# Attention by pairs of heads, masks merged into other operations, the normalisation on ScalarE and all convolution taps on VectorE

## The chip, the cores and the metric

The kernel runs on one core of one Trainium2 chip. The metric is the device time of one execution in microseconds (us). Before the change three runs took 2025.07, 2022.62 and 2021.49 us, a median of 2022.62. Engines are called as in the profile: PE is TensorE's matmuls and PEld its weight loads, DVE is VectorE, ACT is ScalarE, POOL is GpSimd, SP is SyncE.

## The reference

Two layers of a transformer block over 256 tokens `x` and 256 context tokens, width 1024, all in float32. What it computes, without the helpers:

```python
for l in range(DEPTH):
    last = l == DEPTH - 1
    mx, mc = ...                  # nine modulation vectors for x and for the context
    x = x + 0.5 * mx[2] * swiglu(modulate(rms_norm(x, norm_g[l, 0]), mx[0], mx[1]), w_ffn1_gu[l], w_ffn1_down[l])
    ...                           # the same for the context
    zx = modulate(rms_norm(x, norm_g[l, 1]), mx[3], mx[4]) @ w_in[l]
    zc = modulate(rms_norm(h_ctx, norm_g[l, 1]), mc[3], mc[4]) @ w_in[l]
    qa, ka, va, qb, kb, vb, ux, gx = split_combined(zx)
    qa_c, ka_c, va_c, qb_c, kb_c, vb_c, uc, gc = split_combined(zc)
    qb, kb = apply_axial_rope(qb, cos, sin), apply_axial_rope(kb, cos, sin)
    ya = neighborhood_attention(qa, ka, va, ka_c, va_c, na_rpb[l], rows)
    yb = window_attention(qb, kb, vb, kb_c, vb_c, sw_sink[l])
    yc = conformer_conv(ux, conv_dw_w[l], conv_dw_b[l], conv_ln_g[l], conv_ln_b[l])
    x = x + mx[5] * merge_branches(ya, yb, yc, gx, b_gate[l], w_out_a[l], w_out_b[l], w_out_c[l], w_out[l])
    if not last:
        ...                       # context_attention, the same convolution and merge for the context
    x = x + 0.5 * mx[8] * swiglu(modulate(rms_norm(x, norm_g[l, 2]), mx[6], mx[7]), w_ffn2_gu[l], w_ffn2_down[l])
return rms_norm(x, final_g)
```

The change lies in the middle, between `zx` and `merge_branches`. The neighborhood attention has six heads of 64 features; a query sees a window of 8 by 16 places with a bias `na_rpb` and all context keys. The window attention has six query heads on two key heads, sees keys at most 128 tokens away and the context, and has one more logit, `sw_sink`, in the softmax. The convolution is depthwise over 256 channels with 31 taps, then a layer norm over the channels and silu. Each branch goes through its own projection and a sigmoid gate before the common `w_out`.

## The kernel before

Features lie on the 128 partitions and tokens along the columns: 256 of x, then 256 of the context (in the last layer the queries, gates and the convolution are needed for x alone, 256 columns). Every float32 product is made of three matmuls of rounded parts, `hi*hi`, `hi*lo` and `lo*hi` (`mm3`, L317 to L321). The weights come in one stream from DRAM in the order of use; a block of 512 columns, four weight tiles, is split into `wh` by ACT (L125) and `wl` by DVE (L126) shortly before PE needs it.

`middle(l, norm, nxt)` is the middle branch of one layer. Its work on PE, in the order of the program:

- the first blocks: the keys `ka` of the neighborhood heads and the two halves of the convolution's input, which are put into a padded tile (`hp`);
- the values: eight k of twelve products of 512 columns (`v`), each k followed by `CV_PACE[l]` steps of the convolution;
- two queries (`query`), then the loop over units. A unit is a head and `u`: the first or the second 128 queries of x, or, in layer 0, the 256 queries of the context (`u == 2`). For each unit come the scores (`qk`), the softmax (`soft`), later the transposes of the weights (`turn`, 4 products into the bank `pt`) and, after a head's last unit, the products with the values (`pv`). Between them `step(n)` takes n steps from `fill`, a chain of the other blocks of the middle: the third query, the keys and queries of the window heads with their rotation, a few gates, and `merge(b, f)`, which projects branch b (2 is the convolution, 0 the neighborhood heads, 1 the window heads) and multiplies it by its gate. A step is three matmuls. The turn of a unit comes `LOOKAHEAD` units after its scores.

The scores of a head are one product on all 128 rows, which stacks two parts of the key or of the query, and one on 64 rows for the third part (L1024). The softmax takes a maximum on DVE (L1036, L1037 with the mask or bias), the exponential with its sum on ACT (L1057), the reciprocal on DVE (L1066) and the scaling of the weights on POOL (L1068). Biases `tb` come by DMA for each head, and POOL adds the window's mask (L1004).

`conv()` has 62 taps of 31 per half of the channels. 44 are done on DVE (L802, L805), the last 18 of one half on ACT (a product, L811) and POOL (a sum, L815, with a last sum on L817). Then comes its layer norm: the mean (`cmean`, L827), sums of squares (`sums`), the inverse root spread over all rows (`rstd`), scaling, tanh and the split parts `ych` and `ycl`. Work of the norm that waits for other engines is put off by `after(n, fn)` until n further ticks, and `flush()` runs what is left when `fill` needs the result.

A scheduler places the instructions on each engine in an order of its own guess, within what the data allow; the tiles come from rings and pools of fixed size.

Of the kernel before, what the change touches and what calls it, by code (L numbers as in the profile page):

```python
# [39 lines left out]
# columns of the packed vectors  # L40
# [31 lines left out]
LOOKAHEAD = 2  # L72
N_TAP = 6
# [5 lines left out]
N_ROT = 4  # L79
# [3 lines left out]
N_CPOOL = 18  # L83
CV_PACE = (3, 2)
EARLY = (2, 8)
# [4 lines left out]
def dit_block_kernel(ctx, tc, xT, vec, ident_d, const, crow, gfin, rpb, ws, ada0, adaT, out):  # L90
    """Builds the program; returns the 128x128 weight tiles (input, layer, first row, first column)
    in the order in which ws has to hold them."""
# [78 lines left out]
    def mod_chunk(l, ch, ks=slice(0, KD)):  # L171
        """What the chunk of eight feature tiles is for, from the modulation itself."""
# [22 lines left out]
    def ada_first(ch, raws):  # L195
        """A chunk of layer 0's first two, on TensorE, in two halves."""
# [25 lines left out]
    class Ada:  # L222
        """The modulation's other feature tiles, one after the other on VectorE."""
# [41 lines left out]
    class Stream:  # L265
# [14 lines left out]
        def make(self):  # L280
            """Loads and splits the next tiles."""
# [66 lines left out]
    def inv_rms(groups, nq, unit, out, new=S):  # L348
        """inv_root along the columns, on all partitions. In two steps, for TensorE to work in between."""
# [14 lines left out]
    class Norm:  # L364
        """rms_norm(R) * g * (1 + scale) + shift. Its first products are taken of R * g * (1 + scale)
        with the shift as one more column, and scaled by 1/rms afterwards."""
# [76 lines left out]
        def parts(self, p):  # L443
            """(product without its shift, columns, shift) for each set."""
# [53 lines left out]
    class FirstNorm(Norm):  # L498
        """The program's first norm, made while the modulation comes in: its first products are taken
        of all but the shift and 1/rms, and the shift's own product is added afterwards."""  # L500
# [19 lines left out]
        def blocks(self, fns):  # L520
# [54 lines left out]
            # the shift's product: its two parts are the columns of the stationary operand, and a last  # L575
            # product turns the rows into columns and adds the parts
# [36 lines left out]
    def project(l, br, name, xs, sets, nxt, bg=lambda f: 0):  # L613
        """R += gate * (xs @ w), and what the next norm needs of R."""
        for f in range(KD):
# [4 lines left out]
            if f == KD - 2:  # L620
                # the function's table is there before the norm needs it
# [3 lines left out]
    def ffn(l, br, norm, nxt, ada_end=None):  # L625
        """ada_end: how many of the modulation's tiles there have to be at the end."""
# [11 lines left out]
        def bg(i):  # L638
            """The tiles to do now, of 20 pairs of blocks and the first 6 tiles of the projection."""
# [40 lines left out]
    def middle(l, norm, nxt):  # L680
# [7 lines left out]
        def pair(name):  # L688
            """A split tile of the width of qs."""
# [9 lines left out]
        mna = ph[:, C_MNA:C_MNA + GRID_W]  # L699
        msw = ph[:, C_MSW:C_MSW + 2 * NX].rearrange("p (u k) -> p u k", u=2)  # L700
# [6 lines left out]
        # on the first blocks: the keys of the neighborhood heads and one half of the convolution's input  # L707
# [4 lines left out]
        for parts in fb[:3]:  # L712
            # a tile for each head: the one part where its rows are, the rest in the other half
            kt = [S(F32R, "ka") for _ in range(2)]
            for t, sl, b in parts:
                for s, r in enumerate(rows):
                    o = rows[1 - s]
                    nc.scalar.activation(out=kt[s][r, sl], in_=t[r], func=AF.Identity, bias=b[r])
                    nc.vector.scalar_tensor_tensor(
                        out=kt[s][o, sl], in0=t[r], scalar=b[r], in1=f32(kt[s][r, sl]),  # L720
                        op0=ALU.add, op1=ALU.subtract)
            ka.append(kt)
# [26 lines left out]
        # the other half of the convolution's input  # L749
# [587 lines left out]
```

## Time and profile before

| | |
|---|---|
| three runs, median | 2022.62 us (2021.49 to 2025.07) |
| profiled execution, span from the first to the last instruction | 2022.2 us |
| granted TensorE clock over the span, mean | 0.993 |
| middle branch of layer 0 up to its `w_out` | about 441 to 788 us |
| middle branch of layer 1 up to its `w_out` | about 1598 to 1800 us |

No time other than its span is given for the profiled execution. The profile names a group by line, engine, operation and tiles (out<-in), with the count, the busy time and the mean of one. A timeline row is start, length, engine, line, operation, tiles, count and in brackets the idle time before it with what ended it. A matmul's length includes the pipeline's depth, so a series is timed from start to start. The granted clock is the share of full speed that PE had in a stretch.

### The profile page before, as it was taken

What the parts mean: (1) busy time and instruction counts of PE and PEld (TensorE: products, weight loads), DVE (VectorE), ACT (ScalarE), POOL (GpSimd) and SP (SyncE); (2) the same over time, 40 slices, a digit from 0 to 9 for tenths busy, and PEclk for the clock granted to TensorE, in tenths of its full rate; (3) what the DMA queues carried; (4) which work ended last, traced back from release to release, by engine and by line L of the source; (5) the groups of instructions that cost most, each with busy time, mean ns of one, the idle gap of its engine ahead of it and who ended that gap; (6) DMA issues with size and microseconds to landing.
All of it is one profiled execution on the core that took longest, in us unless ns stands there. A gap on an engine that the chain in (4) does not pass through costs nothing.

```text
span 2022.2 us, 29714 instructions
## 1 busy us (share of the span) xinstructions
PE 1973.9 (98%) x10650; PEld 1658.4 (82%) x10650; DVE 1466.8 (73%) x3330; ACT 921.4 (46%) x1828; POOL 222.5 (11%) x220
## 2 busy tenths in 40 slices
PE   7999999997999999999999999999999989999998
PEld 3788888895777788988888888888888978999998
DVE  5887777579976655887667659766774899978654
ACT  4533323355655544543333335333333757767553
POOL 0000000107322200100000010000001233200001
PEclk9999999998999999999999999999999989999999
DMA  7455555421221222254544524544453243355553
GB/s 286 166 191 178 174 178 176 137 83 54 71 98 63 76 92 94 94 188 152 171 156 156 176 96 165 162 157 163 156 166 119 70 130 104 135 180 186 188 184 109
DMA packets 82516, 287.22 MB, mean 142 GB/s; under 512 B 9152, under 2 KB 10944, under 8 KB 81984
## 3 DMA queue, kind: packets, MB, share of 16 engines
q1 hardware_dynamic: 79488, 277.91, 41.5%
q0 software_dynamic: 864, 4.78, 0.6%
q10 hardware_dynamic: 2016, 2.64, 0.5%
q8 instruction: 83, 1.36, 0.3%
q14 instruction: 65, 0.53, 0.1%
HBM read 284.24 MB, written 1.05 MB: 141 GB/s over the span
## 4 chain that ended last, share of the span: by engine, by line
PE 89%; DVE 8%; ACT 1%; issue 1%; POOL 0%; DMA 0%; ACTq 0%; DVEq 0%; POOLq 0%
PE g L320 13%; PE g L319 13%; PE g L321 13%; PE pr L319 8%; PE pr L321 8%; PE pr L320 8%; PE b L321 3%; PE b L319 3%; PE b L320 3%; DVE cacc L805 2%; PE f L319 2%; PE sc L1024 2%; PE f L320 2%; PE f L321 2%; PE pt L1078 1%; DVE wl L126 1%
## 5 line engine op out<-in xcount | busy, mean ns | idle before, releaser
L125 ACT ACTIVATE wh<-raw 128x512 fp32r<-128x512 f32 x760 | 472.8, 629 | 712.1 <-PE g L320 261.7
L126 DVE TENSOR_TENSOR wl<-raw,wh 128x512 fp32r<-128x512 f32 x760 | 533.2, 706 | 166.5 <-PE pr L321 89.5
L246 DVE CUSTOM_DVE_ANT_0 junk<-araw,phase 128x512 f32<-128x512 f32 x512 | 356.1, 696 | 144.8 <-DMA araw<-in_adaT_dram 135.2
L320 PE MATMUL g<-Hl,wh 128*128 128x512 f32 (+1 forms) x1248 | 457.8, 367 | 1.7 <-DVE Hl L480 1.7
L321 PE MATMUL g<-Hh,wl 128*128 128x512 f32 (+1 forms) x1248 | 457.6, 367 | 0.0
L319 PE MATMUL g<-Hh,wh 128*128 128x512 f32 (+1 forms) x1248 | 457.4, 367 | 0.0
L320 PEld LDWEIGHTS g<-Hl,wh 128*128 128x128 f32 x1248 | 234.8, 188 | 43.3 <-DVE Hl L480 2.2
L321 PEld LDWEIGHTS g<-Hh,wl 128*128 128x128 f32 x1248 | 234.5, 188 | 42.0
L319 PEld LDWEIGHTS g<-Hh,wh 128*128 128x128 f32 x1248 | 234.6, 188 | 41.5
L319 PE MATMUL pr<-gh,wh 128*128 128x512 f32 (+1 forms) x704 | 258.5, 367 | 0.0
L321 PE MATMUL pr<-gh,wl 128*128 128x512 f32 (+1 forms) x704 | 257.6, 366 | 0.0
L320 PE MATMUL pr<-gl,wh 128*128 128x512 f32 (+1 forms) x704 | 257.4, 366 | 0.0
L387 POOL TENSOR_TENSOR sq<-sq,sq 128x512 f32<-128x512 f32 (+1 forms) x36 | 44.0, 1222 | 1277.9 <-ACT sq L380 1275.8
L321 PE MATMUL b<-Hh,wl 128*128 128x512 f32 (+1 forms) x480 | 167.7, 349 | 10.6 <-DVE wl L126 10.5
L319 PE MATMUL b<-Hh,wh 128*128 128x512 f32 (+1 forms) x480 | 171.0, 356 | 0.0
L320 PE MATMUL b<-Hl,wh 128*128 128x512 f32 (+1 forms) x480 | 166.4, 347 | 0.0
L321 PEld LDWEIGHTS pr<-gh,wl 128*128 128x128 f32 x704 | 132.4, 188 | 23.5
L320 PEld LDWEIGHTS pr<-gl,wh 128*128 128x128 f32 x704 | 132.4, 188 | 23.2
L319 PEld LDWEIGHTS pr<-gh,wh 128*128 128x128 f32 x704 | 132.4, 188 | 23.0
L319 PE MATMUL f<-qh,wh 128*128 128x258 f32 (+1 forms) x400 | 121.1, 303 | 0.1
L320 PE MATMUL f<-ql,wh 128*128 128x258 f32 (+1 forms) x400 | 116.6, 292 | 0.0
L321 PE MATMUL f<-qh,wl 128*128 128x258 f32 (+1 forms) x400 | 116.5, 291 | 0.0
(234 smaller groups left out, 2819.3 us busy)
## 6 DMA issues: line engine op xcount, KB each, us to landing
raw<-in_ws_dram SPq DMA_DIRECT2D x380, 512.0 KB, 3.4
araw<-in_adaT_dram SPq DMA_DIRECT2D x128, 512.0 KB, 3.9
araw<-in_ada_dram SPq DMA_DIRECT2D x32, 256.0 KB, 5.9
phase<-in_crow_dram POOLq DMA_DIRECT2D x3, 1024.0 KB, 6.0
tb<-in_rpb_dram ACTq DMA_DIRECT2D x12, 192.0 KB, 2.4
R<-in_xT_dram SPq DMA_DIRECT2D x8, 256.0 KB, 5.3
phase<-in_const_dram POOLq DMA_DIRECT2D x2, 544.0 KB, 5.8
out_dram<-fin SPq DMA_DIRECT2D x4, 256.0 KB, 2.5
```

Of the source, the lines that this page charges most:

```text
L125: nc.scalar.activation(out=hi, in_=src, func=AF.Copy)
L126: nc.vector.tensor_tensor(out=lo, in0=src, in1=f32(hi), op=ALU.subtract)
L246: nc.vector.tensor_tensor_reduce(out=junk, in0=raw[:, c], in1=self.rows[:, s, c], scale=1.0, scalar=0.0, op0=ALU.mult, op1=ALU.add, accum_ ...
L319: nc.tensor.matmul(ps, wh, xh, start=start, stop=False)
L320: nc.tensor.matmul(ps, wh, xl, start=False, stop=False)
L321: nc.tensor.matmul(ps, wl, xh, start=False, stop=stop)
L387: eng.tensor_tensor(out=a[:, full], in0=a[:, full], in1=sq[:, full], op=ALU.add)
L805: nc.vector.scalar_tensor_tensor(out=wide(acc), in0=x, scalar=w, in1=wide(acc), op0=ALU.mult, op1=ALU.add)
L1024: nc.tensor.matmul(o, a[:, c], b[:, k], start=i == 0, stop=i == 1)
L1078: nc.tensor.transpose(pt[:, i * P:(i + 1) * P], pf[:, i * P:(i + 1) * P], ident)
```

## The change

The heads are handled in pairs. The query and key of two heads are one split pair of tiles, one head on rows 0 to 63 and one on rows 64 to 127; the scores are three products on 64 rows for each head, with the two heads taking turns into two PSUM banks. There are 216 such products rather than 72 on 128 rows and 72 on 64; the other counts of matmuls stay. Queries are scaled by the negative factor, so a minimum takes the place of the maximum, and the exponential has the scale -1. The neighborhood mask is put into the bias table on the host, and ACT negates the table after its load (L972). For the window heads the mask has zeros for the context, so one operation covers all 512 columns (L1009). The normalisation goes from POOL to ACT (L1032). A pair's transposes come at `u == 1` (16 in a row) and `u == 2` (8), each bank split in one operation of 512 columns; the values' products come for both heads, and the output is split once a pair.

All 62 taps are done on DVE (L788, L791), one step a k beside the values (`CV_V`) and one every second step of `fill` after that (`CV_PACE`). Several gates are made ahead, before the keys and queries of the window heads (`EARLY`: 7 in layer 0, 16 in layer 1), in layer 1 two to a tile. `LOOKAHEAD` goes from 2 to 1. Comments are dropped, which shifts the line numbers.

```diff
-C_MNA = C_SIN + NX
-C_MSW = C_MNA + GRID_W
-C_N = C_MSW + 2 * NX
+C_MSW = C_SIN + NX
+C_N = C_MSW + 3 * NX
...
-LOOKAHEAD = 2
-N_TAP = 6
+LOOKAHEAD = 1
+N_TAP = 3
...
-N_ROT = 4
+N_ROT = 2
...
-N_CPOOL = 18
-CV_PACE = (3, 2)
-EARLY = (2, 8)
+CV_V = (1, 1)
+CV_PACE = (2, 2)
+EARLY = (7, 16)
...
-                if m % 2 and m // 2 < N_CPOOL:
-                    # the last taps of one half, on ScalarE and GpSimd
-                    x, w = tap(1, nv + m // 2)
-                    t = S(name="cside") if side is None else next(taps)
-                    nc.scalar.activation(out=wide(t), in_=x, func=AF.Copy, scale=w)
-                    if side is None:
-                        side = t
+            for j in range(CONV_W):
+                for c in range(2):
+                    acc, o = accs[c], c * CONV_W + j
+                    x, w = hp[:, c, :nst, j:j + NX], cw[:, o:o + 1]
...
-                        nc.gpsimd.tensor_tensor(out=side[:, qs], in0=side[:, qs], in1=t[:, qs], op=ALU.add)
-                yield
-            nc.gpsimd.tensor_tensor(out=accs[1][:, qs], in0=accs[1][:, qs], in1=side[:, qs], op=ALU.add)
+                        nc.vector.scalar_tensor_tensor(
+                            out=wide(acc), in0=x, scalar=w, in1=wide(acc), op0=ALU.mult, op1=ALU.add)
+                    yield
...
-            run(cv, CV_PACE[l])
+            run(cv, CV_V[l])
...
-            # the one part twice for each head, and the rest where its rows are
-            qd, ql = heads_tiles("qd"), S(F32R, "ql")
...
+            qh, ql = pair("q")
+            nc.scalar.activation(out=qh[:, qs], in_=ps[:, qs], func=AF.Copy, scale=-QSCALE)
...
-                    for i, (a, b) in enumerate(terms):
-                        nc.tensor.matmul(o, a[:, c], b[:, k], start=i == 0, stop=i == 1)
+                    for i, (a, b) in enumerate(((qh, kh), (qh, kl), (ql, kh))):
+                        for s, r in enumerate(rows):
+                            nc.tensor.matmul(pss[s][:, o], a[r, c], b[r, k], start=i == 0, stop=i == 2)
...
+                elif u < 2:
+                    v = ps.rearrange("p (n k) -> p n k", n=2)
+                    nc.vector.tensor_tensor_reduce(
+                        out=v, in0=v, in1=msw[:, u::2 - u, :][:, :2], scale=1.0, scalar=nsink[:, h:h + 1],
+                        op0=ALU.add, op1=ALU.min, accum_out=st[:, 0:1],
+                    )
...
-                    nc.gpsimd.tensor_scalar(
-                        out=pf[:, i * w:(i + 1) * w], in0=pf[:, i * w:(i + 1) * w],
-                        scalar1=st[:, 6 + i:7 + i], scalar2=0.0, op0=ALU.mult, op1=ALU.add,
-                    )
+                    c = slice(i * w, (i + 1) * w)
+                    nc.scalar.activation(out=pf[:, c], in_=pf[:, c], func=AF.Copy, scale=st[:, 6 + i:7 + i])
...
         fill = chain(
-            query(2), key_b(), query_b(0), query_b(1), query_b(2),
-            *(gate(2, f) for f in range(EARLY[l])),
+            query(2), *(gate(b, f) for b, f in early),
+            key_b(), query_b(0), query_b(1), query_b(2),
...
+            if 0 <= n - LA < N:
+                us[n - LA][0].turn(us[n - LA][1])
+                tick()
+            if pss:
+                h.soft(u, pss)
+                if u == 1 and us[n][0] is not us[-1][0]:
+                    us[n + nu - 1][0].bias()
...
+            if 0 <= n - LA < N and us[n - LA][1]:
+                us[n - LA][0].pv(us[n - LA][1])
```

What this moves on the engines, at three places. First DVE in layer 0, beside the values: `wl` is the low part of a block of weights, `cacc_3998` and `cacc_3999` are the sums of the two halves of the convolution. Before:

```order
L805 SCALAR_TENSOR_TENSOR cacc_3998<-phase_3439,cw_4000,cacc_3998 128x512
L805 SCALAR_TENSOR_TENSOR cacc_3999<-phase_3439,cw_4000,cacc_3999 128x512
L126 TENSOR_TENSOR wl_4131<-raw_4128,wh_4130 128x512
L805 SCALAR_TENSOR_TENSOR cacc_3999<-phase_3439,cw_4000,cacc_3999 128x512
L805 SCALAR_TENSOR_TENSOR cacc_3998<-phase_3439,cw_4000,cacc_3998 128x512
L805 SCALAR_TENSOR_TENSOR cacc_3999<-phase_3439,cw_4000,cacc_3999 128x512
L805 SCALAR_TENSOR_TENSOR cacc_3998<-phase_3439,cw_4000,cacc_3998 128x512
L805 SCALAR_TENSOR_TENSOR cacc_3999<-phase_3439,cw_4000,cacc_3999 128x512
L126 TENSOR_TENSOR wl_4152<-raw_4128,wh_4151 128x512
```

And now, with the sums called `cacc_3986` and `cacc_3987`:

```order
L125 TENSOR_TENSOR wl_4169<-raw_4166,wh_4168 128x512
L791 SCALAR_TENSOR_TENSOR cacc_3987<-phase_3439,cw_3988,cacc_3987 128x512
L791 SCALAR_TENSOR_TENSOR cacc_3986<-phase_3439,cw_3988,cacc_3986 128x512
L791 SCALAR_TENSOR_TENSOR cacc_3987<-phase_3439,cw_3988,cacc_3987 128x512
L125 TENSOR_TENSOR wl_4173<-raw_4166,wh_4172 128x512
L791 SCALAR_TENSOR_TENSOR cacc_3987<-phase_3439,cw_3988,cacc_3987 128x512
L791 SCALAR_TENSOR_TENSOR cacc_3986<-phase_3439,cw_3988,cacc_3986 128x512
L791 SCALAR_TENSOR_TENSOR cacc_3987<-phase_3439,cw_3988,cacc_3987 128x512
L125 TENSOR_TENSOR wl_4212<-raw_4209,wh_4211 128x512
```

Five taps stood between two splits there; now it is three, at an even pace, though the table of paces asks for one.

Second PE in layer 0 at the convolution's norm: `cmean` is its mean, `b` and `qb` other blocks of the middle, `sc` scores, `pt` transposed weights. Before:

```order
L827 MATMUL cmean_4483<-cacc_3998,onesC 128x512
L827 MATMUL cmean_4483<-cacc_3999,onesC 128x512
L319 MATMUL b_4440<-Hh_3714,wh_4382 128x512
L320 MATMUL b_4440<-Hl_3715,wh_4382 128x512
L321 MATMUL b_4440<-Hh_3714,wl_4383 128x512
L319 MATMUL b_4440<-Hh_3722,wh_4382 128x512
L320 MATMUL b_4440<-Hl_3723,wh_4382 128x512
L321 MATMUL b_4440<-Hh_3722,wl_4383 128x512
L1024 MATMUL sc_4505<-ka_3865,qd_4291 128x512
L1024 MATMUL sc_4505<-ka_3865,ql_4292 128x512
L1078 MATMUL pt_4515<-ident,pf_4215 128x128 x4
```

And now, where `sums` and `rstd` are the norm's next steps and `mo` is the projection of the convolution's branch:

```order
L804 MATMUL cmean_5190<-cacc_3986,onesC 128x512
L804 MATMUL cmean_5190<-cacc_3987,onesC 128x512
L339 MATMUL sums_5197<-onesC,ctap_5170 128x1
L339 MATMUL sums_5197<-onesC,ctap_5171 128x1
...
L358 MATMUL rstd_5213<-ctap_5172,ones 128x512
L318 MATMUL mo_5236<-ych_5220,wh_5040 128x512
L319 MATMUL mo_5236<-ycl_5221,wh_5040 128x512
```

Other blocks stood between the norm's products, with the window heads' queries still to come; now those queries lie ahead, and the four steps stand one behind the other.

Third PE in layer 1 at the window heads: `kd`, `kl` or `kbh`, `kbl` are keys, `qx` queries, `pv` the products with the values. Before, at one unit:

```order
L1024 MATMUL sc_15854<-kd_14436,qx_14672 128x512
L1024 MATMUL sc_15854<-kl_14437,qx_14672 128x512
L1078 MATMUL pt_15866<-ident,pf_14134 128x128 x4
L319 MATMUL mo_15850<-y_14865,wh_15759 128x256
L320 MATMUL mo_15850<-y_14865,wh_15759 128x256
L321 MATMUL mo_15850<-y_14865,wl_15760 128x256
L319 MATMUL mo_15850<-y_15118,wh_15759 128x256
```

And now, at two units of a pair, where the numbers of `sc` tell the heads apart:

```order
L987 MATMUL sc_15260<-kbh_15038,qx_15243 128x512
L987 MATMUL sc_15261<-kbh_15038,qx_15243 128x512
L987 MATMUL sc_15260<-kbl_15039,qx_15243 128x512
L987 MATMUL sc_15261<-kbl_15039,qx_15243 128x512
...
L1048 MATMUL pt_15289<-ident,pf_13952 128x128
L1067 MATMUL pv_15310<-pt_13953,v_13926 128x256
L1067 MATMUL pv_15310<-pt_13954,v_13926 128x256
...
L987 MATMUL sc_15335<-kbh_15038,qx_15243 128x512
L987 MATMUL sc_15336<-kbh_15038,qx_15243 128x512
```

Blocks of the projection stood between the units; now a unit's scores are followed at once by a pair's transposes and value products, and the next unit's scores are mixed in among those.

More of the change, by code (lines that the diff above doesn't have):

```diff
@@ L712, in middle @@
         for parts in fb[:3]:
-            kt = [S(F32R, "ka") for _ in range(2)]
+            kh, kl = S2("ka")
             for t, sl, b in parts:
[L716 to L722, printed above, removed]
+                nc.scalar.activation(out=kh[:, sl], in_=t, func=AF.Identity, bias=b)
+                nc.vector.scalar_tensor_tensor(
+                    out=kl[:, sl], in0=t, scalar=b, in1=f32(kh[:, sl]), op0=ALU.add, op1=ALU.subtract)
+            ka.append((kh, kl))
         sg = S(name="sg")
@@ L921, in key_b @@
             z = rope(ps, 1.0, full)
-            kd, kl = [S(F32R, "kd") for _ in range(2)], S(F32R, "kl")
-            for s, r in enumerate(rows):
-                nc.scalar.activation(out=kd[s][r, full], in_=z[r, full], func=AF.Copy)
-                nc.vector.tensor_copy(kd[s][rows[1 - s], full], f32(kd[s][r, full]))
-                nc.vector.tensor_tensor(
-                    out=kl[r, full], in0=z[r, full], in1=f32(kd[s][r, full]), op=ALU.subtract)
-            kb.append((kd, kl))
+            kh, kl = S2("kb")
+            split(kh[:, full], kl[:, full], z[:, full])
+            kb.append((kh, kl))
         def query_b(j):
@@ L932, in query_b @@
             yield from steps(ps, [W.one("w_in_qb", l, k * P, j) for k in range(KD)], H, qs)
[L933 to L941 removed]
+            z = rope(ps, -QSCALE, qs)
+            qh, ql = pair("qx")
+            split(qh[:, qs], ql[:, qs], z[:, qs])
+            qb.append((qh, ql))
         M = [None] * KD
@@ L947, in gate @@
             pg = yield from block(GT + b * D + f * P, qs)
-            g = S(name="gate")
+            if last and f % 2:
+                g = gates[b, f - 1, 0][:, hc]
+            else:
+                gates[b, f, 0] = S(name="gate")
+                g = gates[b, f, 0][:, qs]
             o = b * KD + f
-            nc.scalar.activation(out=g[:, qs], in_=pg[:, qs], func=AF.Tanh, bias=hb[:, o:o + 1], scale=0.5)
+            nc.scalar.activation(out=g, in_=pg[:, qs], func=AF.Tanh, bias=hb[:, o:o + 1], scale=0.5)
             gates[b, f] = g
@@ L1029, in soft, with soft_one @@
+            def soft(self, u, pss):
+                self.pf[u] = [self.soft_one(u, s, ps) for s, ps in enumerate(pss)]
+            def soft_one(self, u, s, ps):
                 pf = next(pfs)
@@ new lines, in turn @@
+                    return
+                for s in range(2):
+                    if u == 1:
+                        jobs = [("loc", [(u, 0, i) for i in range(2) for u in range(2)]),
+                                ("ctx", [(u, NX, i) for i in range(2) for u in range(2)])]
+                    else:
+                        jobs = [("cc", [(2, q * NX, i) for i in range(2) for q in range(2)])]
+                    for name, parts in jobs:
+                        pt = PS("pt")
+                        for n, (v, o, i) in enumerate(parts):
+                            nc.tensor.transpose(
+                                pt[:, n * P:(n + 1) * P], self.pf[v][s][:, o + i * P:o + (i + 1) * P], ident)
+                        h, lo = next(pts), next(pts)
+                        split(h[:, :NT], lo[:, :NT], pt)
+                        self.p[s][name] = (h, lo)
@@ new lines, in pv @@
+            def pv(self, u):
+                j = 3 if self.kind else self.j
+                if u == 1:
+                    self.po = [PS("pv") for _ in range(2)]
+                sl, jobs = (hx, [("loc", 0), ("ctx", 2)]) if u == 1 else (hc, [("cc", 2)])
+                for s in range(2):
+                    n, m = len(jobs) * 4, 0
+                    for name, t0 in jobs:
+                        for i in range(2):
+                            c = (j % 2 * 2 + s) * P
+                            k = slice(i * NX, (i + 1) * NX)
+                            for p in self.p[s][name]:
+                                nc.tensor.matmul(
+                                    self.po[s][:, sl], V[t0 + i][j // 2][:, c:c + P], p[:, k],
+                                    start=m == 0, stop=m == n - 1)
+                                m += 1
+                if u == nu - 1:
+                    h, lo = pair("y")
+                    y = next(yfs)
+                    for r, po in zip(rows, self.po):
+                        nc.scalar.activation(out=y[r, qs], in_=po[HD:, qs], func=AF.Copy)
+                        nc.vector.tensor_tensor(out=y[r, qs], in0=po[:HD, qs], in1=y[r, qs], op=ALU.add)
+                    split(h[:, qs], lo[:, qs], y[:, qs])
+                    (yb if self.kind else ya).append((h, lo))
+                    npv[0] += 1
```

220 lines of the change are left out of this document (66 added, 154 removed).

## The prediction, made before the change was run

> **What bounds the kernel now.** I read the page's busy times and slices first, then the chain of waits, then what PE waits for in the two middle branches, then tables by stage, and last the timelines of the places that stood out.
>
> ```profile
> PE 1973.9 (98%) x10650; PEld 1658.4 (82%) x10650; DVE 1466.8 (73%) x3330; ACT 921.4 (46%) x1828; POOL 222.5 (11%) x220
> PE   7999999997999999999999999999999989999998
> PEclk9999999998999999999999999999999989999999
> PE 89%; DVE 8%; ACT 1%; issue 1%; POOL 0%; DMA 0%; ACTq 0%; DVEq 0%; POOLq 0%
> ```
>
> TensorE works 98% of the span and carries 89% of the chain that ends last. So the kernel gets faster only by less matmul time, by fewer idle stretches of PE, or by a full clock where it was not full. The two dips (slices 10 and 34 to 35) are where the convolution runs, once in each layer. The waits of PE in the two middle branches (in all, times, longest):
>
> ```profile
> PE b L321 <- DVE wl L126: 9.9, 3, 3.6
> ...
> PE sc L1024 <- ACT qd L901: 8.5, 1, 8.5
> ```
>
> The first row is layer 0, the second layer 1. Four stretches hold the dips, two others are undisturbed (columns: stretch, length, busy time of PE, PEld, DVE, ACT and POOL, granted clock, DMA share, GB/s):
>
> ```profile
> 452.40:498.60 46.20, 35.29 (x135) 27.13 (x134) 46.20 (x52) 20.79 (x43) 35.50 (x18) 0.91 0.14 46
> 498.60:504.30 5.70, 5.68 (x13) 3.82 (x13) 5.67 (x12) 4.18 (x9) 1.81 (x1) 0.51 0.41 133
> 660.00:722.00 62.00, 62.00 (x303) 48.83 (x302) 39.54 (x98) 36.45 (x84) 16.72 (x21) 1.00 0.25 85
> 1606.00:1640.00 34.00, 26.03 (x135) 21.82 (x133) 33.96 (x64) 18.62 (x49) 16.24 (x18) 0.96 0.30 97
> 1640.00:1690.00 50.00, 46.05 (x271) 39.10 (x272) 45.49 (x119) 34.40 (x82) 18.65 (x22) 0.89 0.28 91
> 1720.00:1771.00 51.00, 51.00 (x392) 46.46 (x391) 45.82 (x130) 36.90 (x95) 15.21 (x19) 1.00 0.39 132
> ```
>
> In the first stretch DVE is busy for all of it and PE does 135 matmuls in 46.2 us. DVE is the bound there and POOL works beside it; the timeline shows what that does:
>
> ```profile
> 455.89 6.71 DVE L805 SCALAR_TENSOR_TENSOR cacc<-phase,cw,cacc 128x512 f32<-128x512 f32 x10
> 463.12 8.61 DVE L805 SCALAR_TENSOR_TENSOR cacc<-phase,cw,cacc 128x512 f32<-128x512 f32 x5
> 471.65 1.77 DVE L126 TENSOR_TENSOR wl<-raw,wh 128x512 fp32r<-128x512 f32 x1
> 473.34 5.16 DVE L805 SCALAR_TENSOR_TENSOR cacc<-phase,cw,cacc 128x512 f32<-128x512 f32 x3
> 456.31 35.14 POOL L815 TENSOR_TENSOR cside<-cside,ctap 128x512 f32<-128x512 f32 x17 [6.45 <-ACT ctap L811]
> ```
>
> Ten taps take 6.71 us at first, 0.67 each; a little later three take 5.16, 1.72 each, while POOL adds its side sums, and one weight split takes 1.77. After the idle time the clock is lower for some microseconds:
>
> ```profile
> 498.62 0.80 PE L321 MATMUL b<-Hh,wl 128*128 128x512 f32 x1 [3.63 <-DVE wl L126]
> 499.21 0.63 PE L319 MATMUL b<-Hh,wh 128*128 128x512 f32 x1
> 499.63 0.63 PE L320 MATMUL b<-Hl,wh 128*128 128x512 f32 x1
> ```
>
> After 3.63 us of waiting, matmuls of 512 columns start 0.43 us apart, at a granted clock of 0.51.
>
> **What goes: the stalls of the convolution.** At full clock two such matmuls start 0.23 us apart (the first two rows of the next fence). Layer 0: 135 of them are worth 31.3 us and take 46.2, 13 are worth 3.0 and take 5.7, so 17.6 us are lost. Layer 1, from idle time and clock: 34.00 - 26.03 = 8.0 idle and 4% of 26.0 by the clock; 50.00 - 46.05 = 4.0 idle and 11% of 46.05 by the clock; together 18 us. With POOL's side sums and ACT's products for them gone, DVE has 62 taps rather than 44 plus the join, but at 0.67. The order puts about three taps of layer 0 beside each of the eight k of the values: 0.67 for a split and 3 x 0.67 are 2.7 us on DVE, against 12 matmuls x 0.232 = 2.8 on PE. The cover is thin, but it holds; in layer 1 five or six taps of half the width come to the same. What does not fit stands beside the queries. I count **-36 us** for the two layers and **+2** for the thin cover. If taps take more than 0.72 us, each further 0.1 us costs 8 x 3 x 0.1 = 2.4 us in layer 0.
>
> **The scores.** Three pieces of the timeline, where scores stand between other products:
>
> ```profile
> 609.47 0.39 PE L321 MATMUL b<-Hh,wl 128*128 128x512 f32 x1
> 609.70 0.39 PE L1024 MATMUL sc<-kd,qx 128*128 128x512 f32 x1
> 610.02 0.50 PE L1024 MATMUL sc<-kl,qx 64*128 64x512 f32 x1
> 610.45 0.66 PE L1078 MATMUL pt<-ident,pf 128*128 128x128 f32 x4
> 610.86 0.48 PE L319 MATMUL mo<-ych,wh 128*128 128x512 f32 x1
> ...
> 603.16 1.58 PE L1103 MATMUL pv<-pt,v 128*128 128x256 f32 x12
> 604.58 0.28 PE L1024 MATMUL sc<-ka,qd 128*128 128x256 f32 x1
> ...
> 605.72 0.66 PE L1078 MATMUL pt<-ident,pf 128*128 128x128 f32 x4
> ```
>
> Starts count, not durations. A head's unit of two products takes 610.45 - 609.70 = 0.75 us, 1.50 for a pair; of that 0.46 is work, the rest goes at the passage from 128 rows to 64 and back (0.09 and 0.20). The four products of a context unit take 605.72 - 604.58 = 1.14, 2.28 for a pair. Twelve products of 256 columns take 1.42 us, 0.1185 each. Now a pair has six products on 64 rows, two heads on different halves of the rows, alternating. The trace has no two row halves at work at once. Its nearest row is of products that use a quarter of the columns each:
>
> ```profile
> 32.92 1.08 PE L202 MATMUL ada<-araw,cs 128*32 128x128 f32 x32
> 33.93 0.70 PE L359 MATMUL rstd<-diag,ones 128*128 128x512 f32 x1
> ```
>
> 32 records start within 1.01 us, 0.032 each, where a transpose of the same 128 columns takes 0.103 (four in 0.41 above). Parts of the array do work at once. The bounds: both halves fully at once, 3 x 0.232 + 0.29 = 0.99 us for a pair; one after the other, 6 x 0.232 + 0.29 = 1.68. For a context unit 6 x 0.1185 + 0.3 = 1.01, or 1.72. I take the first, nearest to that row: 24 units save 0.51 and six context units 1.27, 20 us; with 8 or 16 transposes standing together rather than 4, some 40 passages of 0.1 go too. **-24 us**. One after the other it would be 24 x 0.69 + 6 x 0.71 = 21 us less.
>
> The Trainium skill (TensorE: Matmul & The Clock Gate, Part 3: Packing small matmuls) says that products on different row groups run at once, but gives 3.07 times, not four, for four tiles. By that share two tiles would give an estimated 1.54 times, three pairs 0.90 us in place of 0.70, and the sum would come out some 6 us higher, near 1996. No run before the change shows it.
>
> **What is new, the convolution's norm.** In layer 0 before, other blocks stand between the mean's products, the sums, the root's and the output projection. Now the order has them directly one behind the other, since the taps end late and the projection flushes what is put off. The same chain before:
>
> ```profile
> 516.64 1.88 PE L827 MATMUL cmean<-cacc,onesC 128*128 128x512 f32 x4
> ...
> 540.82 0.68 DVE L858 SCALAR_TENSOR_TENSOR ycl<-cacc,ych 128x512 fp32r<-128x512 f32 x1
> ```
>
> It took 24.9 us, spread over other work. Tight, I make it 14 to 15.5: mean 1.9, subtraction and squares 1.9, sums 1.9, root, reciprocal and diagonal 1.7, 1.0 and a copy 0.6, then two halves of six steps on DVE, POOL and ACT of 0.6 to 0.8 each, mostly overlapped, 5.5. PE has 4.2 us of its own in it, so it idles for about 10.5, and after such an idle stretch the clock costs 2.7 as at 498.60. **+13**; between 0 (other work slips in) and 24.9.
>
> **What is new, layer 1's sliding heads.** Sixteen gates made early use up work that stood between the units, and eight steps (24 matmuls) are left for a pair. ACT does its own part of a pair's softmax and now the normalisation too:
>
> ```profile
> L1057 ACT ACTIVATE pf<-sc,st 128x512 f32<-128x512 f32 x24 | 16.4, 684 | 2.6 <-DVE st L1042 1.4 <-DVE st L1046 0.8 <-issue 0.2
> ...
> L1057 ACT ACTIVATION_READ_ACCUMULATOR pf<-sc,st 128x1 f32 x24 | 4.7, 195 | 0.0
> ...
> L1063 ACT ACTIVATE st<-st,vt 128x1 f32<-128x1 f32 x12 | 3.4, 285 | 0.0
> ...
> L125 ACT ACTIVATE wh<-raw 128x512 fp32r<-128x512 f32 x116 | 71.5, 628 | 32.2 <-PE b L320 8.6 <-PE pr L320 6.2 <-DMA raw<-in_ws_dram 5.9
> ```
>
> For a pair: 4 exponentials 3.5, 4 sinks 1.1, 4 scalings at the 0.63 of a split 2.5, 4 splits of weights 2.5, output 1.1, two splits of streamed weights 1.3: 12.0 us. PE: 2.8 for 24 matmuls of 0.1185, 2.0 scores, 16 transposes 1.7, 16 value products 1.9: 8.4. The difference of 3.6 is paid by two of three pairs, as the first has a head start: +7.5, and 1.5 for scores and values mixed by the order: **+9** (0 to 14). In layer 1's neighborhood heads PE has 17 us a pair; ACT at 36.90 of 51.00 has 12.3 of them, and 2.5 for scalings and 1.0 for negating the bias tables bring it to 15.8. It fits on average, but ACT then waits in its own order for the tables' load, with splits and exponentials behind it: **+3.5** (0 to 7). In layer 0 ACT has 25.5 us free of 62.00, which covers all of that. Fewer and wider splits of the turned weights, the mask in one operation and the packed gates lie on DVE and ACT beside PE: nothing. The softmax's path loses POOL's scaling and gains ACT's: nothing but the above.
>
> **The sum**, against the profiled span of 2022.2 us, which stands at the median of the runs shown (2022.62): -36 + 2 - 24 + 13 + 9 + 3.5 = -32.5, **1990 us**.
>
> **The rivals.**
> - *The row halves do not work at once.* For it: the trace never shows it, and its 64-row products cost extra at each passage. Against it: the quarter columns above. +21: **2011**.
> - *The new waits don't come*: PE has work left beside the norm's chain, and ACT's queue stays ahead. For it: the order of instructions says nothing about waits inside ACT, and 17 us a pair were enough before. Against it: nothing stands between the norm's steps. -24: **1966**.
> - *The taps stay dear, and the whole turns out slower.* If 1.72 us a tap came from ACT's or PE's traffic and not from POOL's sums, DVE would need 1.77 + 3 x 1.72 = 6.9 us a k against 2.8: 33 us lost in layer 0 in place of 17.6, and likewise 28 in place of 18 in layer 1; 2022.2 - 24 + 25.5 + 25: **2049**. It is slower than before from about 1.4 us a tap. Against it: 0.67 for the ten taps at 455.89, with PE and ACT at work.
> - *The taps aren't spread*, as the table of paces would have it: the order does pack them beside the values. That is in the forecast already, and costs what the thin cover costs.
>
> **How the numbers follow.** The forecast gets 0.60 (own range 1976 to 2004, from the bounds of the norm, of the sliding heads and of the tiles' share), the serial scores 0.18, no new waits 0.16, dear taps 0.06. The range of 1970 to 2012 leaves out the dear taps, most of the lowest case and the upper part of the serial one. A measurement tells 0.2%, 4 us, from no change: faster 0.91, same 0.03 (from the serial case's upper end), slower 0.06.
>
> **What would show it.** Taps near 0.67 us each, no wait of PE over 1 us in the values, and a clock of 1.0 there (stalls); two score products of a pair starting within some tens of nanoseconds, a pair's unit of about 1.0 us (scores); one idle stretch of about 10 us before layer 0's output projection of the convolution and 0.5 of clock behind it (norm); PE waiting for ACT's `pt` or scaled `pf` late in layer 1, with ACT near 100% busy (sliding heads). The prediction is wrong if scores start 0.23 us apart, or if ACT's scaling takes far more than 0.63 us.

## The result and the profile after

The changed kernel takes 2007.48 us (median of four runs, 2006.36 to 2007.93), against 2022.30 for the kernel before (a fourth run is added to the three above): a ratio of 0.9923, with a 95% interval of 0.9909 to 0.9937. It is faster, by 15 us in place of the 32 that were forecast: inside the forecast range, but with less than half of the gain. The profiled execution has a span of 2004.6 us, 17.6 less than before's, and its parts are compared in what follows. The page, with the busy times, the slices of PE and its clock, and the chain of waits:

```profile
PE 1952.5 (97%) x10722; PEld 1651.6 (82%) x10722; DVE 1411.7 (70%) x3188; ACT 914.7 (46%) x1763; POOL 105.3 (5%) x100
PE   7999999999969999999999999999999998899998
PEclk9999999999979999999999999999999999899999
PE 92%; DVE 3%; ACT 2%; DMA 1%; issue 1%; POOL 1%; ACTq 0%; DVEq 0%; POOLq 0%
```

The dip of slice 10 is gone, and a new one stands in slice 12, at a lower clock. Layer 1's dip stood in slice 33 before (the prediction's "34 to 35" was miscounted) and is in 34 and 35 now. What PE waits for in the two middle branches, layer 0 above and layer 1 below:

```profile
PE sums L339 <- ACT ctap L808: 9.2, 1, 9.2
PE mo L318 <- ACT ych L834: 4.8, 1, 4.8
PE rstd L358 <- DVE ctap L353: 1.6, 1, 1.6
...
PE sc L987 <- ACT qx L124: 10.8, 3, 5.3
```

No wait for `wl` is left. Layer 0 now waits for the convolution's norm, layer 1 three times for the queries of the window heads. Tables by stage (columns as before):

```profile
1692.00:1700.00 8.00, 2.88 (x25) 2.67 (x23) 7.32 (x13) 4.18 (x10) 4.51 (x5) 0.89 0.17 66
1700.00:1712.00 12.00, 11.79 (x65) 9.60 (x66) 9.72 (x25) 8.49 (x22) 0.73 (x1) 0.79 0.15 46
1712.00:1730.00 18.00, 12.55 (x65) 9.52 (x65) 14.91 (x41) 13.52 (x32) 2.62 (x3) 0.78 0.09 30
...
574.00:600.00 26.00, 10.44 (x34) 7.06 (x33) 13.72 (x26) 10.68 (x17) 5.13 (x6) 0.61 0.06 20
440.00:500.00 60.00, 60.00 (x262) 47.54 (x261) 58.71 (x111) 27.54 (x56) 1.31 (x2) 1.00 0.33 109
```

The last row is the stretch that had the stalls before: PE is busy all the time at full clock, DVE for 58.71 of 60 us, POOL hardly at all. The row above it is the norm: PE works 10.44 of 26 us, at a clock of 0.61. The first three rows are the window heads of layer 1: idle time first, then a clock of 0.79 and 0.78 even where PE is busy. The scores of one pair stand in the timeline of PE like this:

```profile
664.40 0.50 PE L987 MATMUL sc<-kbh,qxh 64*128 64x512 f32 x2
664.74 0.39 PE L987 MATMUL sc<-kbl,qxh 64*128 64x512 f32 x2
664.97 0.39 PE L987 MATMUL sc<-kbh,qxl 64*128 64x512 f32 x2
665.30 0.87 PE L1048 MATMUL pt<-ident,pf 128*128 128x128 f32 x6
```

Each row holds the product of both heads. From the first to the transposes it takes 665.30 - 664.40 = 0.90 us, where two heads took 1.50 before.

To find where the 17.6 us come from, each of PE's products in a middle branch is counted up to the start of the next, and these times are added up by the tile that is written. Layer 0 and layer 1 in turn: the stalls at the values, keys and queries (`v` and `b`, in layer 0 also `qb`) -20.2 and -13.7; the scores -17.1 (33.3 to 16.2) and -6.4 (20.5 to 14.1). The norm's products and the projection behind them in layer 0 (`cmean`, `sums`, `rstd`, `mo`) cost +21.8. In layer 1 `qb`, `mo`, `pt` and `pv` together lose +16.2, to the waits for `qx` and at the low clock behind them. The transposes and value products of layer 0 cost +1.8.

### The profile page after: what moved, and what is told of

The parts are those of the page before. It is cut to its first block, busy times and chain, and to the rows that moved or that the text cites. A ratio compares the mean times of both kernels' runs of the same rounds, so it can differ in the third digit from the quotient of the medians.

```text
span 2004.6 us, 29351 instructions
## 1 busy us (share of the span) xinstructions
PE 1952.5 (97%) x10722; PEld 1651.6 (82%) x10722; DVE 1411.7 (70%) x3188; ACT 914.7 (46%) x1763; POOL 105.3 (5%) x100
## 4 chain that ended last, share of the span: by engine, by line
PE 92%; DVE 3%; ACT 2%; DMA 1%; issue 1%; POOL 1%; ACTq 0%; DVEq 0%; POOLq 0%
PE g L319 13%; PE g L320 13%; PE g L318 13%; PE pr L319 8%; PE pr L320 8%; PE pr L318 8%; PE b L318 4%; PE b L319 4%; PE b L320 4%; PE f L318 3%; PE f L319 2%; PE f L320 2%; PE pt L1048 1%; PE sc L987 1%; PE pv L1067 1%; PE mo L318 1%
## 5 line engine op out<-in xcount | busy, mean ns | idle before, releaser
L125 DVE TENSOR_TENSOR wl<-raw,wh 128x512 fp32r<-128x512 f32 x760 | 524.7, 696 | 187.8 <-PE pr L320 80.9
L318 PE MATMUL b<-Hh,wh 128*128 128x512 f32 (+1 forms) x480 | 164.8, 343 | 0.8 <-DVE pt L125 0.7
L320 PE MATMUL b<-Hh,wl 128*128 128x512 f32 (+1 forms) x480 | 162.9, 339 | 0.0
L386 POOL TENSOR_TENSOR sq<-sq,sq 128x512 f32<-128x512 f32 (+1 forms) x36 | 44.1, 1226 | 1278.9 <-ACT sq L379 1276.9
```

The source lines that it names most:

```text
L125: nc.vector.tensor_tensor(out=lo, in0=src, in1=f32(hi), op=ALU.subtract)
L318: nc.tensor.matmul(ps, wh, xh, start=start, stop=False)
L320: nc.tensor.matmul(ps, wl, xh, start=False, stop=stop)
L386: eng.tensor_tensor(out=a[:, full], in0=a[:, full], in1=sq[:, full], op=ALU.add)
```

## The experiments

Three rounds each, against the kernel before on the same chip. The two last columns are the length of the middle branch in the profiled run, from its first product to the first of `w_out`. e1 to e4, e5 to e8 and e9 to e12 ran on three different chips, on which the kernel before had medians of 2022.3, 2023.4 and 2023.7 us; a difference of 1 or 2 us between two groups is therefore not shown.

| kernel | time, us | ratio to before (95%) | layer 0, us | layer 1, us |
|---|---|---|---|---|
| before | 2022 to 2024 | 1 | 372 | 234 |
| the change | 2007.5 | 0.9923 (0.9909 to 0.9937) | 359 | 230 |
| e1, norm earlier | 1990.1 | 0.9840 (0.9825 to 0.9854) | 341 | 229 |
| e2, queries first | 1988.9 | 0.9833 (0.9818 to 0.9847) | 353 | 217 |
| e3, four rotation tiles | 2005.3 | 0.9915 (0.9899 to 0.9932) | 357 | 229 |
| e4, e1 to e3 together | 1976.6 | 0.9772 (0.9757 to 0.9786) | 346 | 214 |
| e5, e4 with layer 0's order | 1975.3 | 0.9763 (0.9749 to 0.9778) | 342 | 215 |
| e6, one head after the other | 2007.6 | 0.9925 (0.9910 to 0.9939) | 359 | 229 |
| e7, before, all taps on DVE | 2027.9 | 1.0023 (1.0014 to 1.0033) | 375 | 235 |
| e8, scaling on POOL | 2004.1 | 0.9905 (0.9890 to 0.9920) | 356 | 228 |
| e9, both heads on one half (second head's scores left out) | 2025.8 | 1.0014 (1.0005 to 1.0023) | 369 | 238 |
| e10, taps as before | 1998.2 | 0.9881 (0.9864 to 0.9897) | 349 | 230 |
| e11, e5 with taps as before | 1992.4 | 0.9852 (0.9837 to 0.9867) | 353 | 221 |
| e12, e5 with scaling on POOL | 1973.8 | 0.9758 (0.9744 to 0.9773) | 339 | 216 |

### e1: the norm of layer 0 earlier

```diff
-CV_PACE = (2, 2)
+CV_PACE = (1, 2)
```

> The change with one number undone in part: in layer 0 a tap at every step of fill rather than at every second, so that the convolution's norm comes while gates are left to compute. Theory A (the norm's chain in layer 0 costs about 20 us because nothing stands between its steps): PE's waits for ctap and ych (9.2 and 4.8 us) go, no half clock behind them, layer 1 as it is; 2007.5 - 20 = about 1988 us. Rival B (the chain's engines are late whatever stands between, and the earlier taps crowd DVE beside the values): the waits move to the values and queries, 2003 to 2010 us.

Measured 1990.1 us, 17.4 less than the change. The timeline of the change in layer 0: DVE's last taps, the mean's product on PE, and the norm's next steps with what stands ahead of them on DVE and ACT:

```profile
512.03 2.07 DVE L791 SCALAR_TENSOR_TENSOR cacc<-phase,cw,cacc 128x512 f32<-128x512 f32 x3
...
572.92 1.88 PE L804 MATMUL cmean<-cacc,onesC 128*128 128x512 f32 x4
...
574.29 1.77 DVE L880 SCALAR_TENSOR_TENSOR rot<-qb,phase 32x256 f32<-32x256 f32 x4 [1.60 <-ACT rot L877]
...
578.79 1.29 DVE L806 TENSOR_TENSOR cacc<-cacc,cmean 128x512 f32<-128x512 f32 x2
...
582.78 0.63 ACT L124 ACTIVATE qxh<-rot 128x512 fp32r<-128x512 f32 x1 [3.33 <-POOL rot L883]
583.32 1.14 ACT L808 ACTIVATE ctap<-cacc 128x512 f32<-128x512 f32 x2
...
583.99 3.67 PE L339 MATMUL sums<-onesC,ctap 128*128 128x1 f32 x16 [9.18 <-ACT ctap L808]
```

The taps are done at 514 us, and the mean waits until 573. The taps don't hold it up: its place in the program does. The generator of the taps is asked once every second step of `fill`, and the mean is queued only when the last tap has been handed out, however early DVE gets to them. With the number at 1 (e1) the taps run as before and the mean comes right behind them:

```profile
510.33 4.06 DVE L791 SCALAR_TENSOR_TENSOR cacc<-phase,cw,cacc 128x512 f32<-128x512 f32 x6
...
527.68 1.88 PE L804 MATMUL cmean<-cacc,onesC 128*128 128x512 f32 x4
```

PE's waits for `ctap` and `ych` are gone, and layer 0 is 17 us shorter. Layer 1 is as it was. Theory A holds; the rival's crowding of DVE did not come.

### e2: window queries ahead of the early gates

```diff
         fill = chain(
-            query(2), *(gate(b, f) for b, f in early),
-            key_b(), query_b(0), query_b(1), query_b(2),
+            query(2), key_b(), query_b(0), query_b(1), query_b(2),
+            *(gate(b, f) for b, f in early),
```

> The change with the order in fill undone: key and queries of the window heads before the early gates, as before the change; the gates stay early. Theory A (the waits of 10.8 us for qx in layer 1 and the half clock behind them come from window queries that are made right before their use): the three waits go and most of the low clock, -15 in layer 1; in layer 0 the norm's chain loses the rotations in its way, -5, and keeps the rest: about 1988 us. Rival B (ACT is behind with the softmax and the normalisation in layer 1, wherever the queries stand): PE then waits for pt or pf in place of qx, 2003 to 2008 us.

Measured 1988.9 us, 18.6 less than the change: 13 in layer 1 and 6 in layer 0. The waits for `qx` are gone. In the change the first of them comes about like this (all engines, layer 1):

```profile
1695.50 0.36 ACT L877 ACTIVATE rot<-qb 128x256 f32<-128x256 f32 x1
...
1697.54 0.86 DVE L880 SCALAR_TENSOR_TENSOR rot<-qb,phase 32x256 f32<-32x256 f32 x2
...
1698.55 1.16 POOL L883 TENSOR_TENSOR rot<-rot,rot 128x256 f32<-128x256 f32 x1 [1.88 <-DVE rot L880]
1699.74 0.42 ACT L124 ACTIVATE qx<-rot 128x256 fp32r<-128x256 f32 x1 [2.23 <-POOL rot L883]
...
1700.21 0.79 PE L987 MATMUL sc<-kbh,qx 64*128 64x512 f32 x2 [5.34 <-ACT qx L124]
```

The rotation passes ACT, DVE, POOL and ACT again, each behind other work in its own queue, and PE has nothing but the scores that need it. With the gates behind the queries the same chain lies beside 16 blocks of gates. The sliding heads of layer 1 then look so in e2:

```profile
1655.00:1690.00 35.00, 33.91 (x277) 31.94 (x275) 25.92 (x65) 32.95 (x75) 0.00 (x0) 1.00 0.37 123
1690.00:1720.00 30.00, 30.00 (x245) 27.79 (x244) 25.32 (x64) 28.06 (x66) 1.54 (x2) 1.00 0.37 121
```

ACT is at 94% in both, which is close, but PE loses only 1.1 us of 65, and the clock is 1.00. Rival B, ACT as the bound of these heads, falls.

### e3: four rotation tiles

```diff
-N_ROT = 2
+N_ROT = 4
```

> The change with the ring of rotation tiles back at four. If the ring of two holds up the next query's rotation (its copy on ACT waits for the query before to be split), the waits for qx in layer 1 fall from 10.8 to about 4 us, layer 0's norm by 4 us: about 1996 us. If the order of fill alone is the cause (theory A in its strict form), the rotations still come right before their use and the time stays within 2004 to 2009 us.

Measured 2005.3 us, 2.2 less. PE's waits for `qx` go from 10.8 to 10.2 us, that for `ctap` from 9.2 to 7.6. The ring of two tiles is a small part at most; the place in `fill` is the cause, as e2 shows.

### e4 and e5: the edits together

```diff
+        window = (key_b(), query_b(0), query_b(1), query_b(2))
+        ahead = tuple(gate(b, f) for b, f in early)
         fill = chain(
-            query(2), *(gate(b, f) for b, f in early),
-            key_b(), query_b(0), query_b(1), query_b(2),
+            query(2), *(window + ahead if last else ahead + window),
```

> The three edits together (a tap at every step in layer 0, window queries ahead of the early gates, four rotation tiles). Theory A: both waits gone, layer 0 -20 and layer 1 -16: about 1971 us. If the two causes overlap or ACT is the bound in layer 1 after all: 1985 to 1995 us.

> As e4_all3, but in layer 0 the early gates stay ahead of the window heads' keys and queries, and only in layer 1 the queries come first. Theory A: in e4_all3 the rotations of layer 0 stand on ACT and DVE ahead of the norm's squares (a wait of 4.3 us and low clock behind it), and with the gates first they come after the norm; layer 0 as in e1_pace1, 341 us, layer 1 as in e4_all3: 1972 us. If the wait comes from the taps' pace and not from the rotations: 1977 us.

e4 takes 1976.6 us, 31 less than the change, with a wait of 4.3 us for `ctap` left in layer 0, since the queries' rotations now stand beside the norm there. e5 keeps the change's order in layer 0 (the diff above, with the two numbers of e1 and e3): 1975.3 us, and the wait for `ctap` is gone. The time falls by 1.3 us of the 4.6 that were expected, and the two chips differ by about as much: layer 0 gets 4 us shorter, to 342, about as in e1, but the profiled span only 0.7.

### e6 and e9: do the two halves of the rows work at once?

```diff
-                    for i, (a, b) in enumerate(((qh, kh), (qh, kl), (ql, kh))):
-                        for s, r in enumerate(rows):
+                    for s, r in enumerate(rows):
+                        for i, (a, b) in enumerate(((qh, kh), (qh, kl), (ql, kh))):
```

> The change with the score products of one head after the other, all three, in place of taking turns between the two halves of the rows; the same products and banks. If the two halves work at once when products take turns (theory A), a unit's pair goes from 0.90 back to about 1.7 us, 30 pairs, +20 us: 2022 to 2030 us. If the gain on the scores came only from fewer passages between 128 and 64 rows (rival), within 5 us of the change: 2005 to 2012 us.

Measured 2007.6 us, the same as the change, which speaks for the rival at first sight. The timeline of PE says otherwise:

```profile
666.57 0.51 PE L987 MATMUL sc<-kbh,qxh 64*128 64x512 f32 x2
666.91 0.40 PE L987 MATMUL sc<-kbl,qxh 64*128 64x512 f32 x2
667.15 0.40 PE L987 MATMUL sc<-kbh,qxl 64*128 64x512 f32 x2
667.47 0.33 PE L1048 MATMUL pt<-ident,pf 128*128 128x128 f32 x1
```

Each name occurs once for each head, and like names still start together (666.572 and 666.582), though the program, also in the order in which it is built for PE, has all three of one head first. So the edit did not make the products serial and told nothing apart. e9 does, with both heads on the same rows; it leaves out the second head's own scores and keeps the number and size of the products:

```diff
-                            nc.tensor.matmul(pss[s][:, o], a[r, c], b[r, k], start=i == 0, stop=i == 2)
+                            nc.tensor.matmul(pss[s][:, o], a[rows[0], c], b[rows[0], k], start=i == 0, stop=i == 2)
```

> The change with both heads' score products on rows 0 to 63: the second head's scores are computed from the first head's query and key, so its own scores are left out; the products are as many and as large. If the scores' gain comes from two halves of the rows at work at once (theory A), a pair's six products come one behind the other, about 0.7 us more in each of 30 units: 2024 to 2030 us. If it came from fewer passages alone (rival): within 5 us of the change, 2005 to 2012 us.

Measured 2025.8 us, 18.3 more than the change. PE's timeline:

```profile
675.05 0.72 PE L987 MATMUL sc<-kbh,qxh 64*128 64x512 f32 x2
675.61 0.62 PE L987 MATMUL sc<-kbl,qxh 64*128 64x512 f32 x2
676.08 0.62 PE L987 MATMUL sc<-kbh,qxl 64*128 64x512 f32 x2
676.63 0.55 PE L1048 MATMUL pt<-ident,pf 128*128 128x128 f32 x3
```

A pair takes 676.63 - 675.05 = 1.58 us in place of 0.90. Without the halves working at once, the change is no faster than the kernel before.

### e7, e10 and e11: the taps alone, and the change without them

e7 is the kernel before with one number changed (and the last sum of the side left out where there is none):

```diff
-N_CPOOL = 18
+N_CPOOL = 0
```

> The kernel before, with one number changed: none of the taps on ACT and POOL, all 62 on DVE. If the taps and weight splits were slow because POOL added its side sums beside them (theory A), the stalls of PE beside the values and queries go in both layers: about 1990 us, taps at 0.7 us. If DVE is simply full there (rival: 18 more taps cost what the sharing cost), PE waits as before or longer: 2018 to 2035 us, taps at 0.7 too but the same waits for wl.

Measured 2027.9 us, 0.2% slower than before. Taps in layer 0, and PE's waits there:

```profile
L805 DVE SCALAR_TENSOR_TENSOR cacc<-phase,cw,cacc 128x512 f32<-128x512 f32 x60 | 43.9, 775 | 0.1
```

```profile
PE sums L340 <- ACT ctap L832: 7.0, 2, 6.8
PE rstd L359 <- DVE ctap L354: 4.7, 1, 4.7
PE cmean L828 <- DVE cacc L805: 1.0, 1, 1.0
```

The same group in layer 0 of the kernel before, for comparison:

```profile
L805 DVE SCALAR_TENSOR_TENSOR cacc<-phase,cw,cacc 128x512 f32<-128x512 f32 x42 | 44.1, 1083 | 0.0
```

Both theories are half right: the time is the rival's, but the waits for `wl` that it expected did not stay. A tap falls from 1083 ns to 775 when POOL and ACT have none, and no wait for `wl` is left in layer 0. But 60 taps take 43.9 us where 42 took 44.1: DVE has as much to do as before, and PE now waits for the norm's steps on ACT and DVE.

e10 and e11 go the other way: in the change, and in e5, the taps as before, at the change's paces (44 on DVE, 18 on ACT and POOL; the diff is that of the change's `conv()`, turned round, with six side tiles).

> The change with the convolution's taps as before: 44 on DVE, 18 on ACT and POOL, at the change's paces. If the taps' move to DVE is what took the stalls away (theory A), taps and splits take up to 1.7 us beside the side sums and PE waits for wl again, about +20 to +30 in both layers, less some of the norm's wait: 2018 to 2035 us. If the even pace and the fewer operand steps on DVE took them away (rival, which the 2028 us of e7 speaks for): 1995 to 2010 us.

> The same edit on e5_best, where neither the norm nor the window queries hold PE up. Theory A: 1990 to 2005 us, with waits for wl beside the values. Rival (DVE has room by the other parts of the change): 1970 to 1980 us.

e10 takes 1998.2 us, 9 less than the change; e11 takes 1992.4, 17 more than e5. DVE and POOL in layer 0 of e10 (timeline):

```profile
485.81 19.87 POOL L810 TENSOR_TENSOR cside<-cside,ctap 128x512 f32<-128x512 f32 x12 [0.99 <-ACT ctap L806]
487.77 5.19 DVE L801 SCALAR_TENSOR_TENSOR cacc<-phase,cw,cacc 128x512 f32<-128x512 f32 x3
```

and PE's longest wait there:

```profile
PE pt L1066 <- ACT pf L1050: 7.6, 1, 7.6
```

The side sums again make three taps take 5.19 us, but beside the first unit and not beside the values. The table of e10 shows the same in two stretches, of which the first holds the values (451 to 474 us):

```profile
440.00:480.00 40.00, 40.00 (x174) 32.32 (x173) 39.55 (x67) 19.97 (x37) 5.95 (x5) 1.00 0.29 95
480.00:520.00 40.00, 31.05 (x145) 24.25 (x144) 36.25 (x51) 25.05 (x52) 24.00 (x15) 0.91 0.27 86
```

PE never stops in the first, with the side sums back in the program; POOL works 5.95 us there, and 24.00 in the second, where PE stands idle for 9 us. So theory A's sign, waits for `wl`, did not come in layer 0 of either run (e11 has one of 0.8 us in layer 1), though e11's time lies in its range; e10's lies in the rival's. The 44 steps of the taps end sooner than 62, so the mean has work around it without e1's edit. That is why the taps' move costs 9 us in the change and saves 17 once the norm is covered anyway.

### e8 and e12: the scaling back on POOL

```diff
-                    nc.scalar.activation(out=pf[:, c], in_=pf[:, c], func=AF.Copy, scale=st[:, 6 + i:7 + i])
+                    nc.gpsimd.tensor_scalar(
+                        out=pf[:, c], in0=pf[:, c], scalar1=st[:, 6 + i:7 + i], scalar2=0.0, op0=ALU.mult, op1=ALU.add)
```

> The change with the normalisation back on POOL. If ACT's extra work were what PE waits for in layer 1 (the forecast's mechanism), the waits for qx shrink and the time falls to 1995 to 2000 us. Theory A (the queries are late by their place): the waits stay, the path over POOL is a little longer, and POOL's scalings beside DVE make some of DVE's work slower: 2007 to 2014 us.

> e5_best with the normalisation on POOL, as before the change. If ACT's queue holds up what is left in e5_best (waits for pf and pt at the first turns): 1969 to 1973 us. If POOL's scalings slow DVE and the path is longer: 1977 to 1985 us.

e8 takes 2004.1 us, 3.4 less than the change, and e12 1973.8, 1.5 less than e5; the runs don't overlap in either case (2002.07 to 2005.21 against 2006.36 to 2007.93; 1973.62 to 1973.89 against 1974.34 to 1975.72). In e8 the waits for `qx` stay at 10.8 us, so ACT's extra work is not what PE waits for in layer 1; in layer 0 the wait for `ctap` falls from 9.2 to 6.1. The intervals of the ratios do overlap, though, so a small loss by the scaling on ACT is likely for e8 and not shown for e12. e8's time lies between the two that were expected: the waits stay, but no slower path shows. e12 has the lowest median, 2.4% below that of the kernel before.

## Why the prediction was right or wrong

- **The stalls, -36 and +2: the size right, the reason half right, so in part luck.** -33.9 was measured. No wait for `wl` is left, and the taps take 746 ns in layer 0:

```profile
L791 DVE SCALAR_TENSOR_TENSOR cacc<-phase,cw,cacc 128x512 f32<-128x512 f32 x60 | 42.3, 746 | 0.1
```

  POOL's side sums do make DVE slow, as the prediction had it (e10's three taps in 5.19 us). But the stalls go without their going, too. In e10, with the sums back, PE's times at `v`, `b` and `qb` in layer 0 still add up to 19.5 us less than in the kernel before, and `b` in layer 1 to 11.9 less: at the change's paces most of the sums stand behind the values. e7 is the other half: the taps' move alone takes 16.1 us from `v` and `b` in layer 0, and gives them back at the window queries (`qb`, +7.5) and at the norm's products (+8.9), since DVE has as much to do as before. So the taps' move clears the values, and the rest of the change clears them without it; the price of the sums is paid where they stand: of the 17 us between e5 and e11 about half lie at `b`, the rest at scores and transposes. How much comes from the paces and how much from the fewer operand steps on DVE, no run tells.
- **The scores, -24: right.** -23.5 was measured, and e9 shows the mechanism by 18.3 us. (The 4 us for passages between transposes can't be told apart in it.) A pair takes 0.90 us, under the lower bound of 0.99 that the prediction took. The share of 3.07 for four tiles, of the Trainium skill (TensorE: Matmul & The Clock Gate, Part 3: Packing small matmuls), gave an estimate of 0.90 us for the three pairs of products alone, with the passages on top. Here 0.90 holds both, so two halves lose nothing that these traces show. The rival of serial halves falls.
- **The norm, +13: the step that failed, first.** It was priced as a chain of 14 to 15.5 us with "the taps end late" as its reason. The taps end at 514 us and the mean stands at 573: the place is that of a count of steps, not of DVE. The chain takes from 572.92 to the projection at 596.08, 23 us, since the rotations of the last two queries stand ahead of its steps on DVE and ACT, and it costs 21.8 by PE's sums and 17.4 by e1. PE waits for 16.0 us of it (9.2, 4.8, 1.6 and 0.4) where the prediction had 10.5. The bound of 24.9 was the better guide than the chain worked out from single steps, in which each engine was taken to be free.
- **Layer 1's window heads, +9: the step that failed, second.** The forecast had ACT 3.6 us behind PE in each pair. In the change ACT is busy 8.49 of 12 and 13.52 of 18 us there, not near 100%, though its scaling takes 0.73 us rather than 0.63; in e2 it is at 94%, and PE hardly waits. What PE waited for was the first rotation and the next two: 10.8 us, and with the low clock behind them +16.2 against the +12.5 of both terms of layer 1. That the two sums are as close as this is luck, since ACT's load was not the cause. The order on record showed the queries' place, moved behind 16 gates; its price was not worked out.
- **The bias tables, +3.5.** No wait of PE over 1 us that leads to them shows in either layer of the change.
- The misses add up: norm 8.8, layer 1 3.7, layer 0's transposes and value products 1.8, scores and stalls 0.6, together 14.9 between the 32.5 that were forecast and the 17.6 of the profiled spans. The other 3 us, from 17.6 to the 14.8 between the medians, come from comparing single executions: the profiled one of the change was the fastest of its four, 1.1 us under their median, and a span of 2022.2 us like that of the profile before goes with a time of 2024.0 in a later run of that kernel, 1.7 above 2022.3. The prediction took that span for one at the median.
- The rival of no new waits (1966) did not come, but e12, with the order mended, is within 8 us of it; the dear taps (2049) did not come either.

## What to carry to other kernels

A step that is paced by counting the program's steps has two effects, when its own engine works and when what follows is queued: look in the trace at the last of its instructions and at the first of the next stage, and if 60 us lie between, as here, the count and not the engine sets the end. When work is moved ahead, what it is moved past loses the cover that it had: follow each producer that stands behind it through all of its engines, with their queues as they are there. And a step that frees an engine brings its gain only when the next stage is covered, so try the parts one by one and together: the same move of the taps cost 9 us in the change and saved 17 in e5.

## What the runs showed of the hardware

In the change, a product on rows 0 to 63 and one on rows 64 to 127 start 3 ns apart (664.401 and 664.404 us), and the third two start 0.23 us after the second two (664.74 and 664.97), which is the pace of single products at full clock; on the same rows, in e9, each single product takes that 0.23 us. So the two halves run beside each other in full. In e6 the second head's first product starts 10 ns after the first head's first and 0.33 us ahead of the first head's second, behind which it stands in the program; whether PE or a step between the program and PE changes the order, no run tells.

In the 26 us of layer 0's norm, waits included, PE's clock was 0.61 on average. In the window heads of layer 1, with waits of 5.3, 1.9 and 3.5 us between, it was 0.78 to 0.89 over 38 us; in e2, where these waits are gone, it was 1.00. There 10.8 of the 16.2 us are waiting and the rest goes with slower work, so in these traces the low clock cost about half as much again as the waits.
